# RWKV's triangular inverse begun ahead of v's projections, its VectorE order pinned, and no large operation left on GpSimd

## The chip, the cores and the metric

One core of a Trainium2 chip runs the whole program. The metric is the device time of one execution in microseconds (us); it is given as the median of three runs. Engines are named as in the profile: PE is TensorE (matmuls), PEld its weight loads, DVE VectorE, ACT ScalarE, POOL GpSimd, SP SyncE, which mostly issues DMAs.

## What is computed

The program is a two-layer network for 256 tokens of width 1024. The change lies in the first layer's mixer alone, which runs an HGRN-2 recurrence over half of the width and an RWKV-7 recurrence over the other half and projects the joined result:

```python
def rwkv7_scan(r, decay, k, v, kk, a):
    def step(state, inp):
        r_t, w_t, k_t, v_t, kk_t, a_t = inp
        sa = jnp.einsum('bhvk,bhk->bhv', state, -kk_t)
        state = (state * w_t[:, :, None, :]
                 + sa[..., None] * (kk_t * a_t)[:, :, None, :]
                 + v_t[..., None] * k_t[:, :, None, :])
        return state, jnp.einsum('bhvk,bhk->bhv', state, r_t)
...
def hgrn_rwkv_mixer(h, w_in, w_out, lb, onorm, mu, w0, w2, a0, a2, g2, k_k, k_a, r_k, ln_w, ln_b):
    u = (h @ w_in).astype(jnp.float32)
    hq, hf, hi, hg, ur = jnp.split(u, [HGRN_WIDTH, 2 * HGRN_WIDTH, 3 * HGRN_WIDTH, HGRN_PROJ], axis=-1)
...
    f = lb + (1.0 - lb) * jax.nn.sigmoid(hf)
    o_a = hgrn2_chunked(heads(jax.nn.silu(hq), HGRN_HEADS), heads(1.0 - f, HGRN_HEADS),
                        heads(hi, HGRN_HEADS), heads(jnp.log(f), HGRN_HEADS))
    o_a = rms_norm(o_a.transpose(0, 2, 1, 3), onorm.reshape(HGRN_HEADS, HGRN_HEAD_DIM))
    o_a = o_a.reshape(B, S, HGRN_WIDTH) * jax.nn.silu(hg)
    ur = ur + (token_shift(ur) - ur) * mu
    r, k, v, wd, ad, gd = jnp.split(...)
...
    y = rwkv7_scan(r4, rh(decay), k4, v4, kk, rh(a))
    y = head_layer_norm(y, ln_w.reshape(RWKV_HEADS, RWKV_HEAD_DIM),
                        ln_b.reshape(RWKV_HEADS, RWKV_HEAD_DIM))
    bonus = jnp.sum(r4 * k4 * r_k.reshape(RWKV_HEADS, RWKV_HEAD_DIM), axis=-1, keepdims=True) * v4
    o_b = (y + bonus).reshape(B, S, RWKV_WIDTH) * g
    return jnp.concatenate([o_a, o_b], axis=-1).astype(h.dtype) @ w_out
```

After the mixer come a feed-forward part, attention, and a second layer with a mixture of experts. They are untouched.

## The kernel before

**Projections.** Features lie on the partitions, tokens along the free axis. A projection takes a slab of the weights of 256 columns (one DMA from SP), and each half of it is split into a rounded high part (cast on ACT, L116) and a remainder (subtraction, L117, on DVE or, where the argument `eng` says so, on POOL). 24 matmuls of 128x256 (L137 to L139: high times high, high times low, low times high) make one half's product, which ACT scales into `ext` and DVE combines with it, shifted by one token (L430). The slabs come in the order k (2), r (2), v (2), then HGRN's E (`hE`, 2), q, i (`hv`), g; v's four halves are called v0 first, v0 second, v1 first, v1 second below.

**RWKV's mixer.** The recurrence is done in chunks of 16 and in blocks of 32 tokens. Products of `bt` and `al` (L556) go through masks into `El` (L558). Its diagonal blocks go through DRAM (`dd` written at L567, `db` read at L569, both from ACT's queue), so that 128 small unit triangular systems lie one to a partition, and `inverse()` solves them on DVE: for each of 31 rows k a multiplication (L650) and a subtraction or addition into `qb` (L652). `qb` then goes to DRAM (L655) and comes back as `qs` (L660, eight small DMAs on SP), is copied into `Ql` (L661) and transposed into `Tu` (L664), four pieces each. `levels()` doubles the blocks with PE products (L684 to L735), and `chain()` runs the chunks one after another (L767, L768), normalizes (`yy`, L781 to L791) and transposes (L788).

**HGRN.** `hE`, `n1` and the logarithms give factors `bc`; a loop over levels l of 0 to 8 masks `zz`, `z2`, `z3` and multiplies them (L865); then the states `ST`, `STx` (L886, L887), the gate g, and the output `oo` (L909), after which the mixer's output projection begins.

**What sets the order.** A scheduler orders each engine's instructions from the code's order. `fills` is a list of generators, `tick()` advances the first; so pieces of RWKV are strewn into HGRN's code. `tc.issue_after(ins)` puts whatever is traced inside it behind `ins` on the same engine. Within an engine the order is fixed once built, so an instruction that waits holds all that stand behind it.

## Time and profile before

| what | value |
|---|---|
| median of 3 runs (lowest to highest) | 1330.45 us (1330.16 to 1331.88) |
| the profiled execution's own time | 1331.68 us |
| its span, first to last instruction | 1329.8 us |
| granted TensorE clock over the span | 0.935 of full speed |
| busy PE | 1164.5 us, 88% of the span |
| busy DVE, ACT, POOL | 717.6, 497.6, 208.1 us (54%, 37%, 16%) |

Busy PE is the time in which any matmul is under way; it counts matmuls at half clock at their longer duration. The mixer that is changed takes about the first 205 us of the span.

### The profile page before, as it was taken

The numbers are of one execution on the slowest core, as the hardware profiler recorded it, in microseconds if no ns is written. First come the engines' busy times: TensorE is split into PE (matmuls) and PEld (weight loads), VectorE is DVE, ScalarE is ACT, GpSimd is POOL, SyncE is SP. The second block draws the span as 40 slices with busy tenths as digits, with TensorE's granted clock in tenths as the row PEclk, the third lists the DMA queues.
The fourth block names the chain that finished last, engine by engine and source line by source line (L and its number), as shares of the span: only waits on it lengthen the run. The fifth ranks groups of instructions, "written<-read, shape, count | busy, mean of one in ns | idle before, by whom it ended". The sixth has DMA issues, their size and how long they took to land.

```text
span 1329.8 us, 18843 instructions
## 1 busy us (share of the span) xinstructions
PE 1164.5 (88%) x7392; PEld 849.3 (64%) x7392; DVE 717.6 (54%) x1293; ACT 497.6 (37%) x870; POOL 208.1 (16%) x218
## 2 busy tenths in 40 slices
PE   8899789999999999999999999898877676777765
PEld 7888787988988888898999888662322121212222
DVE  4768866676777887657665689861112010101112
ACT  7626325454444656546444555620000000000002
POOL 4500010222221351122222232300000000000000
PEclk9899799999999999999999999999987896967797
DMA  8342116768785553667775853699999999999996
GB/s 276 116 119 96 17 65 218 263 240 286 281 291 187 176 184 127 220 232 245 259 246 174 335 190 147 233 366 414 420 422 421 421 420 420 422 418 423 419 422 269
DMA packets 129503, 362.35 MB, mean 272 GB/s; under 512 B 13441, under 2 KB 69505, under 8 KB 105857
## 3 DMA queue, kind: packets, MB, share of 16 engines
q1 hardware_dynamic: 126848, 359.78, 71.9%
q10 hardware_dynamic: 2560, 1.31, 0.4%
q8 instruction: 60, 0.98, 0.3%
q14 instruction: 35, 0.28, 0.1%
HBM read 359.49 MB, written 1.57 MB: 272 GB/s over the span
## 4 chain that ended last, share of the span: by engine, by line
PE 52%; DMA 27%; DVE 11%; issue 4%; ACT 3%; POOL 3%; SPq 0%; ACTq 0%; DVEq 0%; POOLq 0%
DMA ew<-in_exp_w_dram 16%; PE acc L138 9%; PE acc L139 9%; PE acc L137 9%; DMA ew<-in_exp_w2b_dram 8%; PE pb L137 3%; PE pb L139 3%; PE pb L138 3%; DMA wm<-in_mod_w_dram 3%; DVE s L117 2%; PE pb L1733 2%; PE pb L1707 1%; PE pf L1707 1%; PE pb L1699 1%; POOL ul L945 1%
## 5 line engine op out<-in xcount | busy, mean ns | idle before, releaser
L117 DVE TENSOR_TENSOR s<-w,s 128x1024 fp32r<-128x1024 f32 x231 | 294.9, 1280 | 104.8 <-ACT s L116 102.7
L116 ACT CAST s<-w 128x1024 fp32r<-128x1024 f32 x240 | 251.0, 1046 | 129.6 <-PE acc L139 105.0
L137 PE MATMUL pb<-xTh,s 128*128 128x256 f32 x512 | 144.6, 282 | 0.6 <-ACT xTh L147 0.6
L138 PE MATMUL pb<-xTh,s 128*128 128x256 f32 x512 | 144.1, 282 | 0.6 <-DVE s L117 0.6
L139 PE MATMUL pb<-xTl,s 128*128 128x256 f32 x512 | 144.3, 282 | 0.0
L945 POOL TENSOR_TENSOR ul<-u,uh 128x256 fp32r<-128x256 f32 x64 | 88.5, 1382 | 249.2 <-ACT uh L944 249.2
L138 PE MATMUL acc<-s,ul 128*128 128x512 f32 x256 | 100.4, 392 | 1.6 <-POOL ul L945 1.6
L137 PE MATMUL acc<-s,uh 128*128 128x512 f32 x256 | 100.1, 391 | 0.0
L139 PE MATMUL acc<-s,uh 128*128 128x512 f32 x256 | 99.8, 390 | 0.0
L137 PEld LDWEIGHTS pb<-xTh,s 128*128 128x128 f32 x512 | 96.2, 188 | 4.7 <-issue 1.7
L139 PEld LDWEIGHTS pb<-xTl,s 128*128 128x128 f32 x512 | 98.2, 192 | 0.5 <-DVE xTl L148 0.4
L138 PEld LDWEIGHTS pb<-xTh,s 128*128 128x128 f32 x512 | 96.2, 188 | 3.0 <-DVE s L117 1.0
L137 PE MATMUL acc<-xTh,s 128*128 128x256 f32 x320 | 94.3, 296 | 3.2 <-ACT xTh L1228 1.5
L138 PE MATMUL acc<-xTh,s 128*128 128x256 f32 x320 | 92.5, 291 | 3.2 <-POOL s L117 1.9
L139 PE MATMUL acc<-xTl,s 128*128 128x256 f32 x320 | 92.1, 291 | 1.7 <-POOL xTl L389 1.3
L1733 PE MATMUL pb<-ew,big 128*32 128x512 f32 (+1 forms) x544 | 76.4, 680 | 19.0 <-DMA ew<-in_exp_w2b_dram 15.4
L1707 PE MATMUL pb<-ew,big 128*32 128x512 f32 x448 | 68.4, 706 | 27.0 <-DMA ew<-in_exp_w_dram 23.0
L1712 DVE SCALAR_TENSOR_TENSOR big<-big,pb 128x512 f32<-128x512 f32 x8 | 5.5, 688 | 160.2 <-ACT big L1711 160.2
L1707 PE MATMUL pf<-ew,big 128*32 128x512 f32 x448 | 67.6, 714 | 26.3 <-DMA ew<-in_exp_w_dram 26.3
L1573 ACT ACTIVATE big<-pb,mc,gs 128x128 f32<-128x128 f32 x28 | 12.8, 457 | 196.2 <-DVE big L1575 196.2
L316 DVE SCALAR_TENSOR_TENSOR macc<-wm,cond,macc 128x512 f32<-128x512 f32 x84 | 66.0, 808 | 21.3 <-DMA wm<-in_mod_w_dram 21.3
L1766 POOL TENSOR_TENSOR frs<-frs,mhalf 128x1 f32<-128x1 f32 x2 | 1.1, 548 | 437.1 <-DVE frs L1764 437.1
(601 smaller groups left out, 2215.9 us busy)
## 6 DMA issues: line engine op xcount, KB each, us to landing
ew<-in_exp_w_dram SPq DMA_DIRECT2D x128, 1024.0 KB, 19.7
w<-in_w_up_dram SPq DMA_DIRECT2D x32, 1024.0 KB, 5.7
w<-in_w_down_dram SPq DMA_DIRECT2D x32, 1024.0 KB, 5.4
ew<-in_exp_w2a_dram SPq DMA_DIRECT2D x32, 1024.0 KB, 19.8
ew<-in_exp_w2b_dram SPq DMA_DIRECT2D x28, 1024.0 KB, 20.0
wm<-in_mod_w_dram SPq DMA_DIRECT2D x24, 1024.0 KB, 7.8
w<-in_w_in_ar_dram SPq DMA_DIRECT2D x14, 1024.0 KB, 5.3
w<-in_w_qkv_dram SPq DMA_DIRECT2D x12, 1024.0 KB, 5.1
```

Source lines behind the costliest of these rows:

```text
L116: A.copy(hi, src)
L117: (eng or V).tensor_tensor(lo, src, hi, sub)
L137: T.matmul(p, lhs[0], rhs[0], start=start, stop=False)
L138: T.matmul(p, lhs[1], rhs[0], start=False, stop=False)
L139: T.matmul(p, lhs[0], rhs[1], start=False, stop=stop)
L316: V.scalar_tensor_tensor(ac, wq, cond[:, k:k + 1], ac, op0=mult, op1=add)
L945: lows[:] = [G.tensor_tensor(ul, u, uh, sub)]
L1573: A.activation(dst, p, AF.Identity, scale=gs[:, kt:kt + 1], bias=sh[:, kt:kt + 1])
L1699: T.matmul(p[:, i * 128:(i + 1) * 128], x[:, tb, (k0 + i) * 128:(k0 + i + 1) * 128], oo[:, tb, :], start=(tb == 0), stop=(tb == 1))
L1707: T.matmul(p[32 * e:32 * e + 32, :], xg[:, k, 32 * e:32 * e + 32], t[:, e, :], start=(k == 0), stop=(k == KT - 1))
L1712: V.scalar_tensor_tensor(th, th, 1.0, hp[0], op0=add, op1=mult)
L1733: T.matmul(p[32 * e:32 * e + 32, :], ht[:, i, 32 * e:32 * e + 32], t[:, e], start=(i == 0), stop=(i == 3))
```

## The change

Four things, all in `mixer0()`. `VG` goes: the second half's subtraction of k, r and v (six of 128x1024), and `rx*kp`, go from POOL to DVE. The `El` part and its DMAs stand ahead of v's projections, and `inverse()` is the first generator in `fills`, advanced three times at each half of v's second slab (`vproj(1, steps=3)`). `behind(step)` holds each DVE instruction that is traced after every third row of the inverse behind that row. HGRN's level loop starts with `tick(100)` and `chain()` in `fills`, which before came at l == 4.

```diff
--- before.py
+++ after.py
@@ -430,7 +430,6 @@
             V.scalar_tensor_tensor(dst, p, omu[:, t:t + 1], e[:, 0:S], op0=mult, op1=add)
 
 
-        VG = (None, G)
         wa = R.tile([128, S], F32, name="wa")
         gd = R.tile([128, S], F32, name="gd")
         lora = r4([128, 2, 512], "lora")
@@ -443,7 +442,7 @@
         la = w0.tile([128, 2, 4, S], F32, name="la", tag="aTh")
         kkx = w0.tile([128, 2, 4, S], F32, name="kkx", tag="aTl")
         ld, ta, kx, kk = la[:, 0], la[:, 1], kkx[:, 0], kkx[:, 1]
-        kproj = lambda j2: proj(2560 + 256 * j2, lambda i, p: shifted(kx[:, 2 * j2 + i, :], p, 2 + 2 * j2 + i), VG)
+        kproj = lambda j2: proj(2560 + 256 * j2, lambda i, p: shifted(kx[:, 2 * j2 + i, :], p, 2 + 2 * j2 + i))
         kproj(0)
         A.activation(wa[0:64, :], wa[0:64, :], AF.Tanh)
         A.activation(gd, gd, AF.Tanh, scale=0.5)
@@ -494,7 +493,7 @@
 
         rx = r4([128, 4, S], "rx")
         for j2 in range(2):
-            proj(2048 + 256 * j2, lambda i, p: shifted(rx[:, 2 * j2 + i, :], p, 6 + 2 * j2 + i), VG)
+            proj(2048 + 256 * j2, lambda i, p: shifted(rx[:, 2 * j2 + i, :], p, 6 + 2 * j2 + i))
 
         Lc = r4([128, 4, S], "Lc")
         for j in range(4):
@@ -526,14 +525,12 @@
         for m in range(2):
             V.tensor_tensor(bt[m], (ta, kp)[m], Lc, mult)
         hp = (slice(0, 64), slice(64, 128))
-        vx = r4([128, 4, S], "vx")
-        for j2 in range(2):
-            proj(3072 + 256 * j2, lambda i, p: shifted(vx[:, 2 * j2 + i, :], p, 10 + 2 * j2 + i), VG)
+        rh = r4([128, 4, S], "rh")
+        V.tensor_tensor(rh, rx, eL, mult)
+        V.tensor_tensor(rx, rx, kp, mult)
 
         El, Tu = big(w0, "aTh", "El"), big(w0, "aTl", "Tu")
-        Ql = big(wsp[-1], "s", "Ql")
-        for t in (Ql, Tu):
-            G.memset(t, 0.0)
+        G.memset(Tu, 0.0)
         m4 = lambda m, n: m[:, None, :].to_broadcast([128, n, 128])
 
         def part(t, l, s):
@@ -571,9 +568,47 @@
         for h in range(2):
             G.memset(qb[64 * h:64 * h + 64, 16 * h:16 * h + 528].rearrange("p (r c) -> p r c", c=33)[:, :, 0:1], 1.0)
         qm = qb[:, 0:512].rearrange("p (r c) -> p r c", c=16)
-        rh = r4([128, 4, S], "rh")
-        V.tensor_tensor(rh, rx, eL, mult)
-        G.tensor_tensor(rx, rx, kp, mult)
+        vx = r4([128, 4, S], "vx")
+        vproj = lambda j2, **k: proj(3072 + 256 * j2, lambda i, p: shifted(vx[:, 2 * j2 + i, :], p, 10 + 2 * j2 + i), **k)
+        vproj(0)
+        Ql = big(wsp[-1], "s", "Ql")
+        G.memset(Ql, 0.0)
+
+        pin = []
+
+        def behind(step):
+
+            if pin:
+                pin.pop().__exit__(None, None, None)
+            if step is not None:
+                pin.append(tc.issue_after(step.ins))
+                pin[0].__enter__()
+
+        def inverse():
+            for k in range(31):
+                n, w = 31 - k, k // 2 + 1
+                tmp = RW.tile([128, 136], F32, name="inv")
+                t3 = tmp[:, 0:n * w].rearrange("p (r c) -> p r c", c=w)
+                V.tensor_tensor(t3, db[:, k + 1:, k:k + 1].to_broadcast([128, n, w]),
+                                qm[:, k:k + 1, 0:w].to_broadcast([128, n, w]), mult)
+                step = V.tensor_tensor(qm[:, k + 1:, 0:w], qm[:, k + 1:, 0:w], t3, add)
+                if k % 3 == 2:
+                    behind(step)
+                    yield
+            behind(None)
+            nc.sync.dma_start(dd[1].rearrange("h q m r c -> (h q m) r c"), qm)
+            qs = t2([128, 2, 16, 16], "qs")
+            for i in range(4):
+                s = slice(32 * i, 32 * i + 32)
+                for h in range(2):
+                    nc.sync.dma_start(qs[s, h], dd[1][h, i].rearrange("m r c -> r m c"))
+                V.tensor_copy(Ql[s, :, s].rearrange("p m (c h) -> p h m c", h=2), qs[s])
+            for i in range(4):
+                s = slice(32 * i, 32 * i + 32)
+                V.transpose(Tu[s, :, s], Ql[s, :, s])
+
+        fills.append(inverse())
+        vproj(1, steps=3)
 
         vt = r4([128, 2, 512], "vt")
         bkt = r4([128, 2, 512], "bkt")
@@ -640,36 +675,6 @@
                     g = p2[:, i * 256:(i + 1) * 256]
                     A.activation(gt[:, j, :], g, AF.Copy, scale=col("ln_w", j))
                     V.scalar_tensor_tensor(bon[:, j, :], bon[:, j, :], col("ln_b", j), g, op0=add, op1=mult)
-                yield
-
-        def inverse():
...
-        def mixed(a_, b_):
-
-            live = [a_, b_]
-            while live:
-                for g in list(live):
-                    if next(g, g) is g:
-                        live.remove(g)
                 yield
 
         def levels():
@@ -792,7 +797,7 @@
                 split((aR[:, 0, :, bs], aR[:, 1, :, bs]), 0, z)
                 yield
 
-        fills += [mixed(pairs(), inverse()), levels()]
+        fills += [pairs(), levels()]
 
         hE = h4([128, 4, S], "hE")
         n1 = h4([128, 4, S], "n1")
@@ -823,6 +828,8 @@
         zs = [zz[:, 0], zz[:, 1], r4([128, 4, S], "z2"), r4([128, 4, S], "z3")]
         ST, STx = r4([128, 2, 4, 128], "ST"), r4([128, 4, 128], "STx")
         G.memset(ST, 0.0)
+        tick(100)
+        fills.append(chain())
         for l in range(9):
             if l == 0:
                 for b in range(2):
@@ -866,10 +873,6 @@
                     V.copy_predicated(part(ST[:, b], l - 1, 1), half4(lvl[:, l - 1, :], l - 1, 1, 4),
                                       part(p.rearrange("p (h c) -> p h c", h=4), l - 1, 1))
                 tick()
-                if l == 4:
-                    tick(100)
-                    fills.append(chain())
-                    tick(2)
             else:
                 p = psa()
                 for h in range(4):
```

Names of the changed file differ by its line numbers: `El` L553 and L555, the inverse L592 and L594, `Ql` L605, `Tu` L608, `hE` L805, `hq` L821, `n1` L810, HGRN's products L872 and L879, transposed `yy` L793, the states L889 and L890, `oo` L912. The places below are as the built programs have them.

DVE in the changed program ahead of v1 second's subtraction (s_791); L592 and L594 are the inverse's rows, here those from the fifth to the tenth, `eka` and `Ekr` RWKV's masked factors:

```order
L653 TENSOR_TENSOR eka_1028<-pb_1018,cst_191 128x256
L594 TENSOR_TENSOR qb_657<-qb_657,inv_779 128x26x3
L656 TENSOR_TENSOR Ekr0_876<-pb_1018,cst_191 128x2x128
L592 TENSOR_TENSOR inv_782<-db_656,qb_657 128x100
L594 TENSOR_TENSOR qb_657<-qb_657,inv_782 128x25x4
L592 TENSOR_TENSOR inv_785<-db_656,qb_657 128x96
L594 TENSOR_TENSOR qb_657<-qb_657,inv_785 128x24x4
L592 TENSOR_TENSOR inv_788<-db_656,qb_657 128x115
L653 TENSOR_TENSOR eka_1078<-pb_1068,cst_191 128x256
L594 TENSOR_TENSOR qb_657<-qb_657,inv_788 128x23x5
L117 TENSOR_TENSOR s_791<-w_732,s_791 128x1024
L592 TENSOR_TENSOR inv_821<-db_656,qb_657 128x110
```

Before, DVE's rows around v's halves (s_627 is v0 first's split, s_689 v1 first's, whose second halves were POOL's; s_836 and s_924 are `hE`'s):

```order
L117 TENSOR_TENSOR s_627<-w_625,s_627 128x1024
L117 TENSOR_TENSOR s_689<-w_687,s_689 128x1024
L575 TENSOR_TENSOR rh_791<-rx_469,eL_604 128x1024
L430 SCALAR_TENSOR_TENSOR vx_624<-acc_630,omu_202,ext1_195 128x256
L430 SCALAR_TENSOR_TENSOR vx_624<-acc_660,omu_202,ext2_196 128x256
L117 TENSOR_TENSOR s_836<-w_834,s_836 128x1024
L430 SCALAR_TENSOR_TENSOR vx_624<-acc_692,omu_202,ext0_194 128x256
L117 TENSOR_TENSOR s_924<-w_834,s_924 128x1024
```

In the changed program v1 second's subtraction stands behind nine rows of the inverse (18 instructions) and factors of RWKV; before, no row of the inverse stood ahead of any split of v.

PE in the changed program at the same place (acc_794 is v1 second's product, acc_893 and acc_949 are halves of `hE`):

```order
L649 MATMUL pf_1131<-rh_624,bt1_621 128x128
L137 MATMUL acc_893<-xTh_157,s_890 128x256
L639 MATMUL pb_1006<-rh_624,bt0_620 128x128 x4
L137 MATMUL acc_949<-xTh_157,s_946 128x256
L639 MATMUL pb_1007<-rh_624,bt0_620 128x128 x4
L649 MATMUL pb_1018<-al_618,bt1_621 128x128
L649 MATMUL pb_1018<-rh_624,bt1_621 128x128
L649 MATMUL pb_1018<-al_618,bt1_621 128x128
L649 MATMUL pb_1018<-rh_624,bt1_621 128x128
L649 MATMUL pb_1068<-al_618,bt1_621 128x128
L649 MATMUL pb_1068<-rh_624,bt1_621 128x128
L138 MATMUL acc_794<-xTh_157,s_791 128x256
```

The last row needs s_791, and the rows ahead of it do not: all of v1 second and what follows on PE stand behind that subtraction.

DVE in the changed program where `Ql` and `Tu` are made; `n_887` is HGRN's logarithm factor, `hE` and `bc` HGRN's:

```order
L821 SCALAR_TENSOR_TENSOR hq<-th,acc 128x256
L672 TENSOR_TENSOR bon<-pb,vx 128x512
L605 COPY Ql<-qs 32x2x16x16
L810 TENSOR_TENSOR n_887<-hE,n_887 128x1024
L608 STREAM_TRANSPOSE Tu<-Ql 32x16x32
L605 COPY Ql<-qs 32x2x16x16
L815 SCALAR_TENSOR_TENSOR bc<-cst,n_887 128x256
L608 STREAM_TRANSPOSE Tu<-Ql 32x16x32
L605 COPY Ql<-qs 32x2x16x16
L812 TENSOR_SCALAR hE<-hE 128x1024
L608 STREAM_TRANSPOSE Tu<-Ql 32x16x32
L605 COPY Ql<-qs 32x2x16x16
```

and before:

```order
L664 STREAM_TRANSPOSE Tu<-Ql 32x16x32
L661 COPY Ql<-qs 32x2x16x16
L642 SCALAR_TENSOR_TENSOR bon<-bon,cols,pf 128x256
L664 STREAM_TRANSPOSE Tu<-Ql 32x16x32
L661 COPY Ql<-qs 32x2x16x16
L866 COPY_PREDICATED ST<-lvl,acc 128x64x4
L664 STREAM_TRANSPOSE Tu<-Ql 32x16x32
L866 COPY_PREDICATED ST<-lvl,acc 128x32x8
L661 COPY Ql<-qs 32x2x16x16
L866 COPY_PREDICATED ST<-lvl,acc 128x32x8
L664 STREAM_TRANSPOSE Tu<-Ql 32x16x32
```

Before, the four copies and transposes were mixed with RWKV's bonus `bon` and HGRN's `ST`; in the changed program the first copy stands behind `hq` and the second piece behind `n1` (L810).

PE at the mixer's end, first of the changed program, then of before (`yy`'s transposes are L793 and L788; the L137 to L139 rows are gate g's projections):

```order
L872 MATMUL acc<-z_1527 128x128 x8
L793 MATMUL pb<-ident,yy_1669 128x128 x4
L872 MATMUL acc<-z_1528 128x128 x8
L793 MATMUL pb<-ident,yy_1717 128x128 x4
L879 MATMUL acc<-zz 128x128 x4
L890 MATMUL acc<-hv,ST 128x128 x4
L889 MATMUL acc<-hv,STx 128x128
```

```order
L139 MATMUL acc<-xTl,s 128x256
L788 MATMUL pb<-ident,yy_1720 128x128 x4
L137 MATMUL acc<-xTh,s 128x256
L138 MATMUL acc<-xTh,s 128x256
L139 MATMUL acc<-xTl,s 128x256
```

Before, the transposes stood among g's 96 matmuls, which came behind all of HGRN's products; in the changed program both transposes stand between the last level's products (L872, L879), and g's 96 matmuls behind the states, ahead of `oo` alone.

## Rows read from the trace of the kernel before

**Rows 1.** Waits of PE from 20 to 205 us: engine, line, waited for; total, times, longest

```profile
PE pb L684 <- DVE Tu L664: 4.7, 2, 3.3
...
PE pb L788 <- DVE yy L781: 3.4, 2, 2.1
```

**Rows 2.** Busy time by stretch: length, PE, PEld, DVE, ACT, POOL, clock, DMA

```profile
50.50:55.50 5.00, 2.08 (x15) 1.24 (x14) 5.00 (x6) 3.01 (x4) 4.90 (x3) 0.93 0.00 0
55.50:61.60 6.10, 6.10 (x28) 6.10 (x29) 5.44 (x3) 0.00 (x0) 3.80 (x2) 0.50 0.64 190
61.60:92.00 30.40, 29.90 (x268) 27.74 (x269) 18.11 (x36) 10.20 (x15) 4.28 (x5) 1.00 0.43 127
92.00:96.00 4.00, 2.73 (x30) 2.25 (x26) 3.93 (x14) 0.45 (x1) 0.00 (x0) 0.97 0.26 33
96.00:102.60 6.60, 6.60 (x31) 6.37 (x30) 2.69 (x10) 0.34 (x1) 0.00 (x0) 0.50 0.36 139
108.00:132.00 24.00, 22.07 (x144) 19.67 (x143) 22.95 (x56) 14.79 (x21) 0.00 (x0) 1.00 0.41 132
132.00:148.00 16.00, 8.75 (x73) 8.18 (x72) 15.58 (x32) 3.67 (x6) 0.00 (x0) 0.97 0.22 33
148.00:161.00 13.00, 12.97 (x166) 12.23 (x167) 8.70 (x17) 5.36 (x10) 0.00 (x0) 0.51 0.01 3
184.00:192.00 8.00, 4.76 (x40) 4.38 (x38) 4.47 (x9) 2.43 (x4) 4.91 (x6) 1.00 0.00 1
```

**Rows 3.** Timeline: start, duration, engine, line, instruction

```profile
51.98 1.22 DVE L527 TENSOR_TENSOR bt<-kp,Lc 128x1024 f32<-128x1024 f32 x1
...
52.10 0.48 ACT L429 ACTIVATE ext<-acc,cols 128x256 f32<-128x256 f32 x1
...
52.37 3.04 POOL L117 TENSOR_TENSOR s<-w,s 128x1024 fp32r<-128x1024 f32 x1
...
53.52 2.98 DVE L117 TENSOR_TENSOR s<-w,s 128x1024 fp32r<-128x1024 f32 x1
```

**Rows 4.** Timeline of PE, two matmuls of g

```profile
199.92 0.28 PE L137 MATMUL acc<-xTh,s 128*128 128x256 f32 x1
200.03 0.28 PE L138 MATMUL acc<-xTh,s 128*128 128x256 f32 x1
```

**Rows 5.** Instructions of one tile, `db`: least/median/most ns, first and last start

```profile
L650 DVE TENSOR_TENSOR inv<-db,qb x31: 157/255/301, 89.5 to 132.6; 128x126 f32<-128x126 f32 x3, 128x30 f32<-128x30 f32 x2, 128x56 f32<-128x56 f32 x2, 128x78 f32<-128x78 f32 x2
...
L569 ACTq DMA_DIRECT2D db<-dd x2: 503/551/599, 79.2 to 79.7; - x2
...
DMA to landing us min/median/max: 3.3/3.5/3.8
```

**Rows 6.** Timeline of DVE, a split and the inverse's end

```profile
88.35 1.22 DVE L117 TENSOR_TENSOR s<-w,s 128x1024 fp32r<-128x1024 f32 x1
...
133.86 0.17 DVE L652 TENSOR_TENSOR qb<-qb,inv 128x16 f32<-128x16 f32 x1
```

**Rows 7.** Timeline of ACT, a cast and a table load

```profile
78.20 1.05 ACT L116 CAST s<-w 128x1024 fp32r<-128x1024 f32 x1
...
104.91 1.28 ACT L802 ACT_TABLE_LOAD   x1
...
106.20 1.06 ACT L802 ACTIVATE n<-hE 128x1024 f32<-128x1024 f32 x1
```

**Rows 8.** Timeline of SP, the reads of `qs`

```profile
136.08 4.05 SPq L660 DMA_DIRECT2D qs<-dd  x8
```

**Rows 9.** Timeline of DVE, first copy and last transpose

```profile
140.95 0.41 DVE L661 COPY Ql<-qs 32x512 f32<-32x512 f32 x1
...
147.27 0.71 DVE L664 STREAM_TRANSPOSE Tu<-Ql 32x512 f32<-32x512 f32 x1
```

**Rows 10.** Timeline of DVE and PE at the mixer's end

```profile
191.34 0.69 DVE L781 TENSOR_TENSOR yy<-yy,st 128x512 f32<-128x512 f32 x1 [2.24 <-POOL st L157]
...
200.61 1.04 PE L909 MATMUL acc<-ident,oo 128*128 128x128 f32 x8
```

More of the change, by code (lines that the diff above doesn't have):

```diff
@@ L642, in pairs @@
                     V.scalar_tensor_tensor(bon[:, j, :], bon[:, j, :], col("ln_b", j), g, op0=add, op1=mult)
-                yield
-        def inverse():
-            for k in range(31):
-                n, w = 31 - k, k // 2 + 1
-                tmp = RW.tile([128, 136], F32, name="inv")
-                t3 = tmp[:, 0:n * w].rearrange("p (r c) -> p r c", c=w)
-                V.tensor_tensor(t3, db[:, k + 1:, k:k + 1].to_broadcast([128, n, w]),
-                                qm[:, k:k + 1, 0:w].to_broadcast([128, n, w]), mult)
-                V.tensor_tensor(qm[:, k + 1:, 0:w], qm[:, k + 1:, 0:w], t3, add)
-                if k % 3 == 2:
-                    yield
-            nc.sync.dma_start(dd[1].rearrange("h q m r c -> (h q m) r c"), qm)
-            qs = t2([128, 2, 16, 16], "qs")
-            for i in range(4):
-                s = slice(32 * i, 32 * i + 32)
-                for h in range(2):
-                    nc.sync.dma_start(qs[s, h], dd[1][h, i].rearrange("m r c -> r m c"))
-                V.tensor_copy(Ql[s, :, s].rearrange("p m (c h) -> p h m c", h=2), qs[s])
-            for i in range(4):
-                s = slice(32 * i, 32 * i + 32)
-                V.transpose(Tu[s, :, s], Ql[s, :, s])
-        def mixed(a_, b_):
-            live = [a_, b_]
-            while live:
-                for g in list(live):
-                    if next(g, g) is g:
-                        live.remove(g)
                 yield
```

## The prediction

> **What bounds the kernel now.** I read the busy shares first: PE is busy 88% of the span, VectorE 54%. So PE sets the time, and a change that leaves PE's work as it is (this one does: every matmul is still there) can gain or lose in two ways only: time in which PE idles, and time in which PE runs at half clock. The whole working is therefore a ledger of these two for the first 205 us. The mixer's end releases the feed-forward part, whose first matmuls wait for nothing but it, so I take a shift there to pass whole to the end of the span.
>
> Then the waits of PE in the mixer [rows 1]: the two largest, 4.7 us for `Tu`, which the inverse makes, and 3.4 for `yy` at the end. Then stretches [rows 2]. In each row the first number is the stretch's length, the next PE's busy time, and the seventh, behind the five engines, the granted clock. The reader is to see three places where PE idles and then runs at half clock (0.50, the lower of the two levels): 50.5 to 61.6, 92 to 102.6 and 132 to 161. At half clock a 128x256 matmul takes 0.213 us (31 in 6.60), at full clock 0.1145 (the next one starts 0.11 later [rows 4]).
>
> **A. GpSimd's large operations go (50.5 to about 66).** Before, PE idles 5.00 - 2.08 = 2.9 us and then loses 6.10 - 28 x 0.1145 = 2.9 us to the clock [rows 2]. The cause stands in two rows that overlap [rows 3]: GpSimd's subtraction takes 3.04 us, and VectorE's, beside it, 2.98, where the same subtraction alone takes 1.22 [rows 6]. In the changed program VectorE does both at 1.22 one after the other, and the `El` products, which need only `bt`, fill part of the wait. v0 first can start at 54.75: the second `bt` ends at 53.2 (1.22 from 51.98 [rows 3]), then come a combination, which I take at the 0.48 of ACT's scaling beside it [rows 3], and a subtraction less the overlap that VectorE's rows show. PE idles about 1.6 by then, and once more 1.85 for v0 second's subtraction, which VectorE has behind the combination that v0 first ends with. If the clock holds, A is worth 2.9 + 2.9 - 1.6 - 1.85 = 2.35, **+2.4**. Bounds: -0.5 (the clock falls again) to +4.4 (the second wait hides behind factor products).
>
> **B. The inverse ahead of v1 second (66 to about 108).** Three halves of 24 x 0.1145, 1.5 of factor products and the wait of 1.85 put v1 first's end at 54.75 + 8.25 + 1.5 + 1.85 = 66.35. Now the pin works. v1 second's subtraction stands behind nine rows of the inverse, and these behind `db`. The two reads of `db` are issued by ACT behind the scaling of v1 first (0.48) and a cast of 1.05 [rows 7], at 67.9; the second is issued 0.55 later and lands 3.5 after that [rows 5], at 72.0. That is 17.5 us ahead of the first inverse row before, at 89.5 [rows 5]. Then VectorE runs 18 inverse instructions of about 0.255 (the median of the inverse's multiplications [rows 5]; 4.6), factors of 1.6 and a subtraction of 1.22: v1 second starts at about 79.5. Of these 13.1 us PE has 4.1 of work that does not need the split (the `hE` and factor matmuls ahead of it in its order), so it idles 9.0. Every stretch before in which PE idled 2.9, 1.3 or 7.3 us was followed by half clock [rows 2], so I add one of 24 matmuls: 24 x 0.099 = 2.4. Back come the idle 1.27 of 92 to 96, the 6.60 - 31 x 0.1145 = 3.05 behind it and the 0.5 of 61.6 to 92 [rows 2]: the factors there are made earlier now. B is -9.0 - 2.4 + 1.27 + 3.05 + 0.5 = **-6.6**. Bounds: -2 (the `db` read earlier by ACT's slack, no clock loss) to -10 (92 to 102.6 does not come back). If `hE`'s halves could cover the wait, nothing would be lost, but PE's order puts v1 second ahead of all but two of their matmuls.
>
> **C. `Tu` and the levels (108 to about 151).** The inverse ends at about 106 where before its last rows stand at 133.86 [rows 6], because hE0's splits are pinned to its rows and PE is 4 behind. `qb` goes to DRAM, the eight reads take 4.05 to issue [rows 8] and the first could be copied at about 113. But in the changed order the first copy stands behind `hq`, which waits for ACT's tanh, and the second piece behind `n1`, which waits for a logarithm. ACT has two table loads more than before on this way, at 1.28 each [rows 7]. Four copies of 0.41 and transposes of 0.71 [rows 9] with `n1`'s 1.2 between them end `Tu` at about 122.3, against 148.0 before [rows 9]. PE, with `hE` and q done and the other slabs' splits behind these on VectorE, idles 6.4 ahead of that and loses some 3.5 to the clock behind it. Back come before's idle time of 108 to 132 (1.9) and of 132 to 148 (7.25), and what 148 to 161 lost at clock 0.51 [rows 2]: at most half of 12.97, 6.5, of which I take 5.9, since q's and `hv`'s projections now lie between the levels. C is -6.4 - 3.5 + 1.9 + 7.25 + 5.9 = **+5.1**. Bounds: -1 to +9 (no clock loss, no wait for ACT).
>
> In the row of the table load, the load starts at 104.91, lasts 1.28, and the next activation starts at 106.20 [rows 7]: nothing lies between. The Trainium skill (ScalarE: Activation LUTs, What ACT_TABLE_LOAD costs) gives about 1283 ns for the load, which the row agrees with, and some 1380 ns of draining with it, which the row does not show. By the page the two loads would cost 5.3 instead of 2.6 us, and C would be 2.8 less.
>
> **D. The mixer's end (151 to 205).** The chain is no longer last. PE's order ends with the last level's two groups, each followed by a transpose of `yy`, then L879, the states, all of g, and `oo`. `chain()`'s steps for `yy` on VectorE stand ahead of the `z` that L879 takes. I walk them from 182.9: `yy` late by 1.8 for the second transpose, `z` by 4.9 for L879, since the steps of `yy` with GpSimd's small powers between (PE waited 3.4 for them before [rows 1]; `yy` itself waited 2.24 [rows 10]) must pass first. Then g's 96 matmuls (11.0 at 0.1145) follow with nothing beside them. Before, g's matmuls lay over these steps, and PE idled 8.00 - 4.76 = 3.24 [rows 2]. I add 1.5 for handing over from states to g and a piece at lower clock. D is -1.8 - 4.9 + 3.24 - 1.5 = **-5.0**. Bounds: +2 (the steps are done before PE asks) to -10 (half clock through all of g: 96 x 0.099 = 9.5, less what falls away). `oo` ended before at 200.61 + 1.04 = 201.65 [rows 10].
>
> **The sum.** +2.4 - 6.6 + 5.1 - 5.0 = -4.1, so 4.1 us slower: 1331.68 + 4.1 = 1335.8 for an execution like the profiled one. That one lies 1.2 above the median of the runs shown, so against the median 1334.6.
>
> **The rivals.**
> Full clock and a `z` in time (faster). The clock falls in none of the three new idle times (+2.4, +3.5) and `z` is ready when L879 asks (+4.9). For it: 184 to 192 kept 1.00 through 3.24 us of idle time [rows 2]. Against: three other stretches fell. With all of these 10.8 the sum is +6.7 and the time 1323.8; with most of them about 1325. It decides when the last level's `z` ends by about 183.5.
> The chain leads (faster). RWKV's chain would end some 10 us earlier, as `Tu` is 25 earlier; if the mixer's end follows it, 1321. Against: PE's work did not shrink, and PE's idle time before, all that can be won, is some 25 us with the clock's, of which the new waits take most.
> Gains and stalls cancel (same): B's wait is shorter by 4, as when `db` lands before v1 first ends: 1330.5.
> The stall of v1 second is longer and the clock stays low in g (slower, further): 1340. For it: nothing stands beside g any more.
> The change doesn't do what it says: the inverse starts early, but the way through ACT's tanh and table loads holds `Tu` to 126 or later. The waits of C are then 3.5 longer: 1338; it counts with the case before.
>
> **How the numbers follow.** Slower by about 4: 0.33. Slower further (1338 to 1340): 0.19. Cancelling: 0.20. Faster, by clock and `z`: 0.20; by the chain: 0.08. The time predicted is the likeliest, 1334.6. For 8 in 10 I leave out the chain's lowest and the far end of the bounds: 1323 to 1343; as signs on both sides hold much of the chance, the likeliest case's own range is 1331.5 to 1339. 0.2%, 2.7 us, is about what a measurement of this kernel can tell from no change; so faster 0.28, same 0.20, slower 0.52.
>
> **What would show it.** A: no GpSimd subtraction around 52, both VectorE splits at 1.2, clock 1.0 from 54 to 66. B: PE's longest wait is for L117 behind the inverse, 6 to 10 us near 70 to 80, with half clock behind it. C: the last transpose ends near 122, PE waits for `Tu` some 6 us and the levels are over before 152. D: L879 waits for `z`, and `oo` ends near 205.5 instead of 201.65. Wrong it would be if B's wait were under 5 us, if the clock stayed at 1.00 behind the waits, or if L879 did not wait.

## The result, and the profile after

The changed kernel takes 1342.79 us in the median of six runs (1339.15 to 1344.25), the kernel before 1331.56 in six runs on the same chip (1330.16 to 1335.54). The ratio is 1.0075 with a 95% interval of 1.0056 to 1.0093: slower, by 0.75%, about 10 us (the medians are 11.2 apart), where 1334.6 and 4.1 us had been forecast. The profiled execution took 1339.21 us with a span of 1337.4, so it shows 7.5 of these 10 us; it is among the fastest of the six.

All of the 7.5 us lie in the mixer. Its last matmuls (`oo`) ended before at 201.65 [rows 10]. In the changed kernel they end at 209.09 + 1.04 = 210.13, 8.5 us later, and the rest of the program takes 1127.3 us against 1128.2. I call this point **the mixer's end** below. It is read from one trace of each kernel, so nothing is built on differences of under 1 us, and where times of many executions say something else, that is said.

The busy times by stretch from the changed kernel's trace (columns as in [rows 2]), the last row for the whole mixer:

```profile
50.50:66.00 15.50, 14.15 (x118) 13.12 (x118) 11.99 (x16) 3.63 (x6) 1.88 (x4) 1.00 0.32 86
66.00:108.00 42.00, 37.26 (x256) 33.59 (x255) 30.34 (x89) 8.66 (x12) 0.00 (x0) 0.84 0.30 85
108.00:151.00 43.00, 36.57 (x337) 31.18 (x337) 31.73 (x52) 27.06 (x39) 0.96 (x1) 0.84 0.39 115
151.00:210.13 59.13, 51.15 (x413) 49.88 (x411) 41.85 (x72) 18.98 (x25) 6.61 (x8) 0.91 0.14 49
0.00:210.13 210.13, 183.93 (x1440) 169.53 (x1440) 149.22 (x286) 99.74 (x154) 18.68 (x36) 0.91 0.37 113
```

The same stretches of the kernel before, to its own mixer's end:

```profile
50.50:66.00 15.50, 12.58 (x81) 11.74 (x81) 12.06 (x11) 4.91 (x7) 12.98 (x8) 0.78 0.44 136
66.00:108.00 42.00, 40.23 (x323) 37.05 (x322) 28.02 (x70) 14.39 (x19) 0.96 (x1) 0.92 0.33 95
108.00:151.00 43.00, 33.79 (x271) 30.82 (x270) 41.52 (x91) 19.89 (x28) 0.00 (x0) 0.95 0.31 86
151.00:201.65 50.65, 47.23 (x458) 45.50 (x455) 33.72 (x57) 17.57 (x27) 6.14 (x8) 0.90 0.16 53
0.00:201.65 201.65, 178.94 (x1440) 167.39 (x1440) 144.16 (x279) 97.33 (x152) 38.79 (x43) 0.93 0.38 116
```

Idle time of PE is length less busy time: in the whole mixer 26.2 us after and 22.7 before. Busy time is 183.9 against 178.9 for the same 1440 matmuls, and the granted clock 0.91 against 0.93. So 3.5 of the 8.5 us are more waiting, and 5.0 are the same matmuls taking longer. These 5.0 are not more time at half clock: PE is busy at clock 0.50 for 9.94 + 10.25 + 5.80 = 26.0 us in the rows that follow, and was for 6.10 + 6.60 + 12.97 = 25.7 before [rows 2]. The mean clock is lower because 11.6 of the 37.55 us in these rows are idle.

```profile
71.28:84.93 13.65, 9.94 (x44) 9.09 (x43) 10.23 (x35) 0.00 (x0) 0.00 (x0) 0.50 0.24 70
119.06:132.72 13.66, 10.25 (x108) 8.73 (x109) 10.19 (x16) 5.09 (x10) 0.00 (x0) 0.50 0.02 3
187.33:197.57 10.24, 5.80 (x27) 5.83 (x28) 5.53 (x9) 3.69 (x5) 0.20 (x1) 0.50 0.00 1
```

What grew are RWKV's factor products: the 96 matmuls of L639 and L649 keep PE busy for 16.2 us, and the same ones for 10.1 before (L604, L614). By stretch, the first is better than before (idle 1.35 instead of 2.92, clock 1.00 instead of 0.78), the second much worse (4.74 instead of 1.77, 0.84 instead of 0.92), and the last one waits for 8.0.

What PE waits for, from 20 to 215 us of the changed kernel (total, times, longest), which answers to [rows 1]:

```profile
PE pb L689 <- DVE Tu L608: 6.1, 2, 4.4
PE acc L879 <- DVE zz L866: 4.7, 1, 4.7
PE pb L793 <- DVE yy L786: 3.3, 1, 3.3
PE acc L138 <- DVE s L117: 2.4, 2, 1.8
```

### The profile page after: what moved, and what is told of

It is laid out like the page before. It is cut to its first block, busy times and chain, and to the rows that moved or that the text cites. A ratio compares the mean times of both kernels' runs of the same rounds, so it can differ in the third digit from the quotient of the medians.

```text
span 1337.4 us, 18829 instructions
## 1 busy us (share of the span) xinstructions
PE 1167.7 (87%) x7392; PEld 850.7 (64%) x7392; DVE 721.2 (54%) x1300; ACT 499.9 (37%) x872; POOL 191.1 (14%) x211
## 4 chain that ended last, share of the span: by engine, by line
PE 50%; DMA 31%; DVE 9%; ACT 4%; issue 4%; POOL 2%; SPq 0%; ACTq 0%; DVEq 0%; POOLq 0%
DMA ew<-in_exp_w_dram 18%; DMA ew<-in_exp_w2b_dram 10%; PE acc L138 10%; PE acc L137 9%; PE acc L139 9%; PE pb L137 3%; PE pb L139 3%; PE pb L138 3%; DMA wm<-in_mod_w_dram 2%; DVE s L117 2%; PE pb L1736 1%; ACT s L116 1%; PE pb L1710 1%; POOL ul L948 1%; PE pf L1710 1%
## 5 line engine op out<-in xcount | busy, mean ns | idle before, releaser
L117 DVE TENSOR_TENSOR s<-w,s 128x1024 fp32r<-128x1024 f32 x237 | 295.4, 1250 | 106.4 <-ACT s L116 105.9
L137 PE MATMUL pb<-xTh,s 128*128 128x256 f32 x512 | 144.5, 282 | 0.6 <-ACT xTh L147 0.6
L139 PE MATMUL pb<-xTl,s 128*128 128x256 f32 x512 | 144.1, 282 | 0.0
L137 PE MATMUL acc<-s,uh 128*128 128x512 f32 x256 | 100.1, 391 | 0.0
L139 PE MATMUL acc<-s,uh 128*128 128x512 f32 x256 | 99.7, 389 | 0.0
L137 PEld LDWEIGHTS pb<-xTh,s 128*128 128x128 f32 x512 | 96.2, 188 | 4.8 <-issue 1.7
L139 PEld LDWEIGHTS pb<-xTl,s 128*128 128x128 f32 x512 | 98.1, 192 | 0.5 <-DVE xTl L148 0.4
L137 PE MATMUL acc<-xTh,s 128*128 128x256 f32 x320 | 93.7, 294 | 3.8 <-ACT xTh L1231 1.5
L139 PE MATMUL acc<-xTl,s 128*128 128x256 f32 x320 | 90.4, 286 | 1.4 <-POOL xTl L389 1.3
L316 DVE SCALAR_TENSOR_TENSOR macc<-wm,cond,macc 128x512 f32<-128x512 f32 x84 | 66.6, 814 | 20.9 <-DMA wm<-in_mod_w_dram 20.9
L1739 DVE TENSOR_TENSOR big<-pb,gate 128x512 f32<-128x512 f32 (+1 forms) x17 | 11.2, 660 | 107.1 <-PE pb L1736 107.1
```

What stands on the lines that cost most here:

```text
L117: (eng or V).tensor_tensor(lo, src, hi, sub)
L137: T.matmul(p, lhs[0], rhs[0], start=start, stop=False)
L139: T.matmul(p, lhs[0], rhs[1], start=False, stop=stop)
L316: V.scalar_tensor_tensor(ac, wq, cond[:, k:k + 1], ac, op0=mult, op1=add)
L1739: V.tensor_tensor(y, p, gate2[:, c:c + n], mult)
```

## How each step of the prediction shows up

**A.** The rows that answer to [rows 3], a subtraction on VectorE and the matmul that waits for it:

```profile
52.72 1.21 DVE L117 TENSOR_TENSOR s<-w,s 128x1024 fp32r<-128x1024 f32 x1
...
53.98 0.38 PE L138 MATMUL acc<-xTh,s 128*128 128x256 f32 x1 [0.61 <-DVE s L117]
```

VectorE's subtraction takes 1.21 where it took 2.98 beside GpSimd's, and v0 first starts at 53.98 (forecast 54.75). The clock is 1.00 through this stretch, as A assumed. PE idles only 1.35 us in it where A had 1.6 + 1.85, since the second wait does not show.

**B.** The timeline of VectorE and PE around v1 second, with the idle time ahead of an instruction and its releaser in brackets:

```profile
71.28 0.21 DVE L592 TENSOR_TENSOR inv<-db,qb 128x31 f32<-128x31 f32 x1 [0.37 <-DMA db<-dd]
...
73.55 0.79 PE L649 MATMUL pb<-al,bt 64*128 64x128 f32 x2 [0.78 <-DVE Ebr L642]
...
75.65 0.42 DVE L653 TENSOR_TENSOR eka<-pb,cst 128x256 f32<-128x256 f32 x1 [0.96 <-PE pb L649]
...
79.31 1.22 DVE L117 TENSOR_TENSOR s<-w,s 128x1024 fp32r<-128x1024 f32 x1
...
80.58 0.58 PE L138 MATMUL acc<-xTh,s 128*128 128x256 f32 x1 [1.84 <-DVE s L117]
```

`db` lands for a first row at 71.28 (forecast 72.0), and v1 second starts at 80.58 (79.5). The reader is to see a mutual wait that the prediction had not walked: rows of the inverse stand on VectorE behind a mask (`eka` at 75.65) that waits for PE's factor products, and those wait for VectorE's masks and already run at half clock, 0.79 for the first pair. So PE idles less than the 9.0 forecast, 4.2 from 66 to 80.6 and 1.84 of it for L117, but does its few matmuls slowly. The half clock does not begin behind the wait, as forecast, but at 71.28, ahead of it: from 66.00 to there PE is busy for 4.81 of 5.28 us, and its only idle time is 0.47.

**C.** The inverse's last row, the first copy, `n1`, the last transpose, and PE's matmul behind it:

```profile
106.37 0.18 DVE L594 TENSOR_TENSOR qb<-qb,inv 128x16 f32<-128x16 f32 x1
...
115.39 0.41 DVE L605 COPY Ql<-qs 32x512 f32<-32x512 f32 x1
...
116.57 1.23 DVE L810 TENSOR_TENSOR n<-hE,n 128x1024 f32<-128x1024 f32 x1 [0.78 <-ACT hE L809]
...
123.43 0.71 DVE L608 STREAM_TRANSPOSE Tu<-Ql 32x512 f32<-32x512 f32 x1
...
124.19 3.62 PE L689 MATMUL pb<-Tu,El 64*64 64x32 f32 x60 [1.65 <-DVE Tu L608]
```

The inverse ends at 106.5 (106), and `Tu` is complete at 124.14 (122.3): the copy does stand behind `hq` and the second piece behind `n1`. But `hq` is not what holds the copy. It is done at 113.5; the copy needs the first two reads of `qs`, which land at 113.3 and 114.3, and stands behind `bon` as well, which waits 1.28 for PE and starts at 114.78.

**D.** The mixer's end in the timeline, and the stretch behind L879's wait:

```profile
185.66 0.69 DVE L786 TENSOR_TENSOR yy<-yy,st 128x512 f32<-128x512 f32 x1 [1.83 <-POOL st L157]
...
186.41 0.66 PE L793 MATMUL pb<-ident,yy 128*128 128x128 f32 x4 [3.27 <-DVE yy L786]
...
190.94 0.68 DVE L866 TENSOR_TENSOR zz<-zz,hq 128x512 f32<-128x512 f32 x1
...
191.77 2.04 PE L879 MATMUL acc<-zz 128*128 128x128 f32 x8 [4.71 <-DVE zz L866]
...
209.09 1.04 PE L912 MATMUL acc<-ident,oo 128*128 128x128 f32 x8
```

```profile
191.80:198.00 6.20, 6.20 (x31) 6.20 (x32) 1.82 (x2) 2.13 (x3) 0.59 (x2) 0.53 0.04 5
```

Both waits of D are there, 3.27 for `yy` and 4.71 for the last level's `zz`, whose mask on VectorE ends at 191.6, behind `yy`'s steps. Behind them PE runs 6.2 us at clock 0.53. Then g's 96 matmuls take the 11 us forecast, at full clock.

ACT's rows between, with one of the table loads that the prediction weighed:

```profile
110.28 1.06 ACT L807 ACTIVATE n<-hE 128x1024 f32<-128x1024 f32 x1
111.36 1.28 ACT L820 ACT_TABLE_LOAD   x1
112.65 0.38 ACT L820 ACTIVATE th<-acc 128x256 f32<-128x256 f32 x1
```

The load takes 1.28 us, starts 0.02 us behind the end of the activation ahead of it, and the next activation starts 0.01 us behind its own end. The Trainium skill (ScalarE: Activation LUTs, What ACT_TABLE_LOAD costs) has some 1380 ns of draining with each switch; these rows agree with its 1283 ns for the load and show no such drain. C's price for a load, 1.28, is what the rows show.

## Experiments

Each is timed in five rounds against the kernel before on the same chip. The mixer's end is from its own trace, to be compared with 201.65 and 210.13. By the ratios most kernels lie 1 to 4 us further below the change than by the mixer's end, 5 and 10 some 4.5 us, and 6 no further.

| kernel | ratio to before, 95% interval | median, us | mixer's end, us |
|---|---|---|---|
| the change | 1.0075 (1.0056 to 1.0093) | 1342.79 | 210.13 |
| 1 GpSimd's part alone | 0.9983 (0.9967 to 1.0000) | 1331.21 | 201.39 |
| 2 change, chain at l == 4 | 1.0002 (0.9988 to 1.0017) | 1334.18 | 202.57 |
| 3 change, `yy` late | 1.0019 (1.0001 to 1.0036) | 1334.28 | 204.67 |
| 4 chain moved alone | 0.9984 (0.9963 to 1.0005) | 1329.68 | 199.16 |
| 5 change, v1 first | 1.0021 (1.0004 to 1.0037) | 1336.57 | 207.22 |
| 6 both 2 and 5 | 1.0003 (0.9980 to 1.0026) | 1333.10 | 200.42 |
| 7 change without pins | 0.9937 (0.9916 to 0.9959) | 1324.06 | 193.18 |
| 8 without pins, chain at l == 4 | 0.9920 (0.9901 to 0.9939) | 1321.37 | 192.31 |
| 9 pins on the first nine rows only | 0.9983 (0.9966 to 1.0000) | 1330.05 | 200.86 |
| 10 pins on the later rows only | 1.0021 (1.0006 to 1.0036) | 1336.17 | 207.59 |
| 11 as 8, GpSimd's splits back | 0.9970 (0.9953 to 0.9988) | 1328.72 | 197.11 |
| 12 as 8, `db` by GpSimd's queue | 0.9925 (0.9906 to 0.9943) | 1322.98 | 193.04 |

My theory at the start was the prediction's: v1 second's wait and the mixer's end are the losses, GpSimd's part a small gain. Its rival was that the losses hand over to each other.

**1. GpSimd's part alone.** The kernel before with

```diff
-        VG = (None, G)
-        kproj = lambda j2: proj(..., VG)
+        kproj = lambda j2: proj(...)
...
-        G.tensor_tensor(rx, rx, kp, mult)
+        V.tensor_tensor(rx, rx, kp, mult)
```

and `VG` left out of r's and v's projections likewise. 

> The kernel before with GpSimd's part alone: the six subtractions of k, r and v and rx*kp on VectorE, all else as before. Theory (a split on GpSimd and one on VectorE that overlap take 3.0 us each, and PE falls to half clock behind that wait): PE's 2.9 us of idle time near 52 and the half clock of 55.5 to 61.6 go, two subtractions of 1.2 us each take their place, and the time falls by 2 to 4 us. Rival (VectorE cannot take 7.3 us more of subtractions in this stretch): the waits for VectorE grow, and the time rises by 1 to 4 us.

Measured: 0.17% faster, 2.3 us, at the edge of its interval, and a mixer's end 0.3 us earlier. A stretch of its trace, then one more and the same of the kernel before:

```profile
50.00:66.00 16.00, 14.97 (x112) 13.85 (x112) 14.05 (x17) 6.47 (x10) 4.40 (x5) 0.89 0.41 132
130.00:170.00 40.00, 34.66 (x305) 32.88 (x306) 26.93 (x53) 11.90 (x19) 0.00 (x0) 0.62 0.07 8
```

```profile
130.00:170.00 40.00, 32.72 (x353) 30.98 (x352) 33.51 (x68) 14.59 (x23) 0.00 (x0) 0.83 0.09 14
```

From 50 to 66 PE works 14.97 of 16 us (13.08 in the same stretch before), so the gain is made; but from 130 to 170, around the wait for `Tu`, the clock is 0.62 instead of 0.83, and the gain is given back there. The theory holds for the place. Its 2 to 4 us are in the time at best, and not at the mixer's end; why the clock stays low longer was not tried.

**2. The chain back at l == 4.** The changed kernel with

```diff
-        tick(100)
-        fills.append(chain())
         for l in range(9):
...
                 tick()
+                if l == 4:
+                    tick(100)
+                    fills.append(chain())
+                    tick(2)
```

> The changed kernel with RWKV's chain put back into the level loop at l == 4. Theory (the mixer's end is made of the waits for yy and for the last level's zz, 3.3 and 4.7 us, and of the half clock behind them): both waits and the half clock near 191 to 197 go, g's projections cover the chain's last steps again, and the time falls by 6 to 9 us against the changed kernel, to 2 to 5 us above the kernel before. Rival (the mixer's end was late already, since the inverse and Tu put all behind by some 4 us, and the chain only shows it): 0 to 3 us against the changed kernel.

Measured: the mixer's end 7.6 us earlier than with the change, the time that of the kernel before. Of the end's waits one is left:

```profile
PE pb L793 <- DVE yy L786: 2.3, 2, 2.1
```

No wait for `zz`: its masks end at 176.1 now, ahead of `yy`'s steps on VectorE. The theory holds; the time fell further than it said, which was 2 to 5 us above the kernel before.

**3. An early chain with late `yy`.** Only the chain's last four steps are moved behind the loop:

```diff
-                tick()
+                if l < 4:
+                    tick()
```

> The changed kernel with the chain begun where the change puts it, ahead of the level loop, but advanced in the loop only for l below 4: its four recurrence steps stay early, its four steps for yy and z come behind the loop, with g. Theory (not the early chain costs, but that the steps of yy stand on VectorE ahead of the last level's zz, with g's 96 matmuls behind both on PE): PE's waits for yy and zz of 8.0 us fall to under 3, the mixer ends at 201 to 203 instead of 210.1, and the time falls by 6 to 9 us against the changed kernel, as with the chain at l == 4. Rival (the chain's matmuls, put ahead of the levels, hold HGRN's levels and so zz): 0 to 3 us.

Measured: 5.5 us of the 7.6 come back at the mixer's end, and the wait for `zz` is gone. So most of it is `yy`'s place ahead of `zz`, not the chain's early start, as the theory said; the mixer's end is 1.7 later than the theory's range allows, with 3.1 us of waiting for `yy` left.

**4. The chain moved alone**, in the kernel before (the lines of 2 the other way round). 

> The kernel before with the chain's start alone moved ahead of the level loop. Theory (the move costs only where Tu is early enough that the whole chain runs inside the levels; here Tu ends near 148, so the transposes of yy stay among g's matmuls in PE's order): the mixer ends within 2 us of the kernel before's 201.7, and the time is the same within 3 us. Rival (the move costs by itself): 5 to 9 us slower than the kernel before.

Measured: the same within the interval, the mixer's end 2.5 us earlier, a little more than the 2 allowed. The move does no harm by itself.

**5. v's second slab ahead of the inverse.**

```diff
-        fills.append(inverse())
-        vproj(1, steps=3)
+        vproj(1)
+        fills.append(inverse())
+        tick(6)
```

> The changed kernel with both halves of v's second slab traced ahead of the inverse, which is then advanced six times at once, its rows pinned as before. Theory (v1 second's split waits behind nine rows of the inverse): PE's idle time of 70 to 80.6 shrinks from 3.6 us and the slow factor products at half clock to under 2 us, the matmuls of 80 to 85 at half clock run at full clock, and the time falls by 5 to 9 us against the changed kernel. Rival (the stall only hands over to the next wait, for Tu, which comes no earlier): PE waits 4 us or more longer ahead of Tu near 116, and the time falls by less than 3 us.

Measured: the mixer's end only 2.9 us earlier than with the change. Waits of PE:

```profile
PE pb L690 <- DVE Tu L608: 10.3, 1, 10.3
```

The stall near 75 is gone, and the wait for `Tu` grew from 6.1 to 10.3, as the rival said: the stall hands over. Its bound on the time does not hold. By the ratios (1.0021 and 1.0075) the time fell by 7 us, inside the theory's 5 to 9, so how much is handed over stays open between 3 and 7 us.

**6. Both edits, 2 and 5.** 

> Both edits together: v's second slab ahead of the inverse, and the chain in the level loop at l == 4. Theory: the two losses stand apart and add up, 11 to 17 us below the changed kernel, so 2 to 7 us below the kernel before. Rival (both edits free the same late work): no more than the better of the two alone, plus 2 us.

Measured: at the mixer's end 9.7 us below the change; the single edits gave 7.6 and 2.9, so there they add up nearly. In time the pair is that of the kernel before, as experiment 2 alone is (1.0003 and 1.0002), so the second edit adds nothing to it. That is the rival's side; the theory's 11 us are not reached. PE waits 9.6 us for `Tu` here. This wait was the open point: the inverse ends early, and PE still has nothing to do.

**7. No pins.** The changed kernel with

```diff
-                pin.append(tc.issue_after(step.ins))
-                pin[0].__enter__()
+                pass
```

> The changed kernel without the pins: nothing is held behind the inverse's rows, all else as changed. VectorE's order then has v1 second's subtraction ahead of the inverse and three of hE's splits among its first rows. Theory (the pins make the stall of 70 to 80 and free nothing later): PE's idle and half clock there go, the inverse ends 1 to 6 us later than 106.4, and the time falls by 2 to 5 us against the changed kernel, the end's 8 us staying. Rival (the pins bring the inverse's end forward by more than the stall costs): Tu comes 8 us or more later and the time rises by 2 us or more.

Measured: 0.63% faster than the kernel before, and the mixer's end 17 us earlier than with the change. Neither side had this. The rival was right on the inverse: it ends at 118.4 instead of 106.5 and `Tu` at 132.5 instead of 124.1.

```profile
118.19 0.17 DVE L593 TENSOR_TENSOR qb<-qb,inv 128x16 f32<-128x16 f32 x1
...
131.81 0.71 DVE L607 STREAM_TRANSPOSE Tu<-Ql 32x512 f32<-32x512 f32 x1
```

But the time did not follow. Stretches of this kernel, and then of the changed one:

```profile
66.00:90.00 24.00, 23.50 (x224) 22.29 (x222) 18.60 (x47) 10.85 (x14) 0.00 (x0) 1.00 0.64 194
90.00:110.00 20.00, 19.21 (x145) 18.00 (x146) 19.79 (x54) 11.81 (x17) 0.96 (x1) 1.00 0.17 54
110.00:130.00 20.00, 19.53 (x117) 16.48 (x115) 19.41 (x40) 10.48 (x15) 0.00 (x0) 1.00 0.51 132
```

```profile
66.00:90.00 24.00, 19.55 (x105) 16.58 (x103) 15.31 (x49) 5.42 (x8) 0.00 (x0) 0.72 0.25 66
90.00:110.00 20.00, 19.70 (x169) 18.71 (x168) 15.57 (x44) 5.22 (x5) 0.00 (x0) 1.00 0.43 137
110.00:130.00 20.00, 13.57 (x142) 11.93 (x142) 13.54 (x24) 13.88 (x21) 0.96 (x1) 0.73 0.24 49
```

Without the pins PE is busy 62.2 of these 64 us at clock 1.00; with them 52.8 at 0.72, 1.00 and 0.73. So my theory, that the pins cost a stall and free nothing, fell on its size. The new one: the pins hold back the splits of hE, q and hv, and these products are what PE could do while the inverse runs and its result goes through DRAM. The traces agree: behind 124.2 the changed kernel still has 94 matmuls of projections (L137 to L139) ahead of g, this one none.

**8. No pins, and the chain at l == 4.** 

> The changed kernel without the pins and with the chain at l == 4: of the change only GpSimd's part and the inverse's place in the code are left. Theory: the stall of 70 to 80 and the end's waits both go; 9 to 14 us below the changed kernel, 0 to 4 below the kernel before, about as GpSimd's part alone. Rival (without pins the inverse is late again and PE waits for Tu as before): within 2 us of the kernel before.

Measured: 0.80% faster than the kernel before, 10.7 us: the best version here, better than both kernels. Stretches of its trace:

```profile
66.00:108.00 42.00, 40.49 (x356) 38.20 (x355) 36.62 (x96) 21.48 (x28) 0.96 (x1) 1.00 0.44 133
108.00:151.00 43.00, 38.85 (x339) 34.94 (x337) 34.47 (x68) 17.92 (x28) 0.00 (x0) 0.77 0.23 62
0.00:192.31 192.31, 177.37 (x1440) 166.84 (x1440) 146.24 (x286) 96.96 (x152) 18.96 (x36) 0.93 0.41 123
```

Idle time is 14.9 us of 192.3, against 22.7 of 201.7 before. The theory's 0 to 4 us below the kernel before was far too small. Without pins the chain's place matters by 0.9 us at the mixer's end, with them by 7.6 (by the ratios 2 and 10): the losses depend on each other.

**9 and 10. Half the pins each.** The pin behind every third row up to the ninth, or only behind the later ones:

```diff
-                    behind(step)
+                    behind(step if k <= 8 else None)
```

and `k > 8` in the other. 

> The changed kernel with the pins of the first nine rows alone: v1 second's subtraction is still held behind the ninth row, hE's splits are free. Theory (a pin costs only if PE has no other product ready; hE's splits, now ahead of the held one, fill the 13 us in which PE idled): no wait over 2 us near 70 to 80, clock 1.00 there, the mixer ends at 192 to 197, 13 us or more below the changed kernel. Rival (v1 second held back is the loss, whatever lies beside it): PE waits for L117 or for v as before, and the mixer ends above 203.

> The other half: no pins on the first nine rows, v1 second is free, all later pins stand, so that hE's splits stay behind the inverse. Theory (hE, q and hv are what PE could do while the inverse runs and its result goes through DRAM; held behind the inverse they leave PE idle ahead of Tu): the stall of 70 to 80 goes but PE idles 6 us or more ahead of Tu, half clock follows, and the mixer ends at 203 to 208, as with both halves of v1 ahead of the inverse. Rival (only the first pin costs): the mixer ends below 198.

Measured with the first pins alone: from 70 to 80, where PE idled, it is busy throughout at full clock, as the theory said (half clock comes later, at 86). The mixer's end is at 200.86, 9.3 us below the change, less than the theory's 13; PE now waits 5.9 us for the last level's `zz`:

```profile
70.00:80.00 10.00, 10.00 (x77) 9.13 (x78) 7.04 (x18) 2.15 (x3) 0.00 (x0) 1.00 0.43 125
```

```profile
PE acc L879 <- DVE zz L866: 5.9, 1, 5.9
```

Measured with the later pins alone: 207.59, inside the theory's range, and PE waits for `Tu`:

```profile
PE pb L689 <- DVE Tu L608: 9.2, 1, 9.2
```

So freeing hE's splits is worth 9.3 and freeing v1 second's 2.5, and both together 17.0; by the ratios it is 12, 7 and 18. The pins on hE are the larger loss by both, as the new theory says; that a held v1 second is harmless once hE is free it had wrong, since freeing it too gives 6 to 8 us more.

**11. The best version with GpSimd's splits back** (the lines of 1 undone in 8). 

> The version without pins and with the chain at l == 4, but with the six subtractions and rx*kp back on GpSimd: of the change only the inverse's place is left. Theory (the order brings the gain and GpSimd's part adds 2 to 5 us): PE's wait near 52 and the half clock of 55 to 62 are back, the mixer ends at 194 to 198, and the time lies 3 to 7 us below the kernel before. Rival (GpSimd's part is the gain): as the kernel before, within 2 us.

Measured: 0.30% faster than the kernel before, the mixer's end 4.8 us later than in 8, both as the theory said. PE waits for GpSimd's subtraction again:

```profile
PE acc L138 <- POOL s L117: 1.2, 1, 1.2
```

GpSimd's part is worth 0.3 us at the mixer's end in the old order and 4.8 in the new one (by the ratios 2.3 and 6.7). What keeps it in the new order was not tried.

**12. `El`'s way through DRAM on GpSimd's queue**, in 8:

```diff
-            nc.scalar.dma_start(dd[0][i]...)
+            nc.gpsimd.dma_start(dd[0][i]...)
```

and `db`'s reads likewise. 

> The version without pins and with the chain at l == 4, with El's way through DRAM (the writes of dd and the reads of db) issued by GpSimd's queue in place of ACT's, where the reads stand behind v1 first's scaling and a cast. Theory (the inverse waits 2.6 us for db, and PE 4 us for Tu): the reads are issued 3 us or more earlier, the inverse ends earlier by about as much, and the time falls by 1 to 4 us against the same version on ACT's queue. Rival (GpSimd's issue takes longer and shares VectorE's time, or PE's waits are set elsewhere): the same within 2 us, or slower.

Measured: no gain; the mixer's end is 0.7 us later. GpSimd's timeline:

```profile
70.74 0.66 POOL L564 DMA_DIRECT2D dd<-El  x1 [3.00 <-DMA dd<-El]
...
75.90 1.06 POOL L566 DMA_DIRECT2D db<-dd  x2 [4.50 <-DMA dd<-El]
```

The four writes are issued over 12 us, from 59.48 on, and the reads at 75.90, 9 us later than from ACT's queue in 8 (66.6). The rival holds.

## Why the prediction was right, and where it was short

The sign was right, and so was the order that makes it: v1 second waits behind nine rows, `Tu` comes behind `n1`, the last level's `zz` behind `yy`. The size was not. About 10 us were lost where 4.1 had been forecast; the time lies outside the likeliest case's 1331.5 to 1339 and inside the range to 1343 by only 0.2 us, which is luck. The milestones follow the walk: 71.3, 80.6, 106.5 and 124.1 us against 72.0, 79.5, 106 and 122.3. The mixer's end did not: 210.1 against 205.5.

A's clock held at 1.00, and A came out at its upper bound: PE idles 1.35 instead of 2.92 and no half clock follows, some 4.5 us by the ledger instead of 2.4. B named a wait of under 5 us as a sign of being wrong, and that sign is there: 1.84 for L117, 4.2 of idle time in all. The step that failed in B is how PE spends the time, not how long it takes. VectorE's rows set when v1 second starts, as walked; PE meanwhile does its factor products, for which 4.1 us had been set down, in small groups between waits and partly at half clock. The ledger knew idle time and half clock only, and these matmuls' longer time has no place in it. C: PE waits 6.1 for `Tu` (6.4), which is 1.8 late.

**D was the term that was mis-sized.** It had 1.8 and 4.9 of waiting and 1.5 for hand-overs and clock, less the 3.24 of before: -5.0. Measured are 3.27 and 4.71, and 6.2 us at clock 0.53, of which I estimate 2.9 as lost: -7.6. By the walk the whole miss at the mixer's end arises here. PE begins to wait for the second `yy` at 183.14, and the walk set out from 182.9, so the 1.8 us of `Tu` have been made good by then. From 182.9 the two forecast waits, the transposes (0.65) and what stands behind L879's start (18.36 us, less the 2.9) lead to an estimated 205.7. From there to 210.1 it is 0.2 of a later start, 1.3 of more waiting and the 2.9 of half clock, which had been named only as a bound and as part of the 1.5. By the sum, which has that 1.5, D is short by 2.6 of the 4.4, and no row places the other 1.8 in A, B or C. What lies between the 7.5 us of the profiled executions and the 10 of the ratio is not explained by this trace; it falls within the runs' own spread.

Of the rivals, that the clock stays at full speed behind the waits is refuted, three times. That RWKV's chain leads is refuted too: `Tu` came 24 us earlier and the mixer ended 8.5 later. Cancelling had a wait of B that is shorter by 4 for its condition; the idle time was shorter by 4.8, and the time did not follow, since v1 second started no earlier. That the stall is longer and the clock stays low came nearest in time (1340); but PE idled less in the stall, g ran at full clock, and the low clock lay ahead of it.

The prediction did not weigh the change against the same kernel without pins, though B says that nothing would be lost if `hE`'s halves could cover the wait; experiment 9 bears that out for 70 to 80. The place of the inverse in the code is worth 4.5 us at the mixer's end by itself (experiment 11) and about 9 together with GpSimd's part (8). The pins cost 17 us with the early chain (7 against the change) and 10 with the chain at l == 4 (8 against 2).

## What to carry to other kernels

Starting a dependent chain earlier pays only with work that the engine behind it has left: the same inverse that ends 12 us later, without pins, gives a mixer that ends 17 us earlier, because PE then does hE, q and hv meanwhile (experiments 7, 9 and 10). When an instruction is pinned, list what PE could do if it were not held, and look for the stretch in which that work is missing. Price a wait of PE with the half clock behind it, and look at the loss one edit at a time and in pairs: the chain's place cost 7.6 us with the pins and 0.9 without. A wait that shrinks is no gain if the next one grows: with v1 second free, the wait for `Tu` went from 6.1 to 10.3. And idle time and half clock are not all that PE can lose: matmuls in small groups between short waits count as busy and take longer, 16.2 us instead of 10.1 for the factor products here, in part at half clock.
